# Splitting the attention branch's input pair by pair, sigmoids in pairs, and new memory offsets in a hybrid encoder layer

## The chip, the core and the metric

The kernel runs on one core of a Trainium2 chip. A core has five engines that work at the same time, each with its own queue of instructions: TensorE (PE; its weight loads are shown apart as PEld), VectorE (DVE), ScalarE (ACT), GpSimd (POOL) and SyncE (SP, which here only issues DMAs). They wait for one another on semaphores. Operands of TensorE lie in SBUF, a memory of 128 partitions; its results go to PSUM, of which this kernel uses eight banks of 128 x 512 float32. The metric is the device time of one execution in microseconds; lower is better.

## What is computed

One layer of a bidirectional hybrid encoder on x of 512 tokens by 1024 channels, in float32:

```python
proj = u @ w_in
q, k, v, z, xbc, dt_raw, gate = jnp.split(proj, offs, axis=-1)
ya = neighbourhood_attention(q, k, v, rpb) @ w_attn_br      # 16 heads of 64
...
ys = y.reshape(bsz, s, D_INNER) @ w_ssd_br                  # two directions of Mamba-2
gates = jax.nn.sigmoid(gate + b_gate).reshape(bsz, s, N_BRANCH, D_MODEL)
merged = gates[:, :, 0] * ya + gates[:, :, 1] * ys
mix = merged @ w_o
...
h = layer_norm(DN_ALPHA * h + mix, ln1_g, ln1_b)
h = layer_norm(DN_ALPHA * h + jnp.square(jax.nn.relu(h @ w1)) @ w2, ln2_g, ln2_b)
```

Here u is a first layer norm of x. Attention works on a grid of 8 rows by 64 columns of tokens: each query sees a window of 8 rows by 16 columns, with a bias from rpb.

## The kernel before

**Products in three parts.** TensorE multiplies in a format shorter than float32, so each operand is split into a high part (a copy into that format, on ScalarE) and a low part (the difference, on VectorE or GpSimd), and each product is three matmuls: high by high, high by low, low by high (`mm3`, L352 to L354). `weights` and `split_weights` (L326 to L350) load a slab of weights (tag `ws`) and split it into `wh` and `wl`, in two halves, two buffers of each tag. In names, h and l at the end stand for the two parts: aTh and aTl, hTh and hTl, mgh and mgl.

**Stages.** The first layer norm and the SSD branch run to 498 us; their order is written by a planner (`Plan`, `slab`, `z_project`, `group_slabs`), which sorts operations by costs and due times. What follows is ordered by a tile scheduler from the order of the code and the buffers: the projection of v (498 to 555 us), the 16 attention heads in eight pairs, the projection of the attention branch (`ps_abr`, 718 to 758 us), gates and merge, w_o, the second layer norm, and the feed-forward (from about 854 us), whose second product uses Strassen's scheme and loads the squared activations `sq..h` and `sq..l` as its stationary operand.

**The heads** (loop over `pr`, L1147 to L1265). Each pair projects q and k, copies them into qf, qs, kf, kh and klz, and then does two heads. For a head: scores into two banks (`pss`), maximum with bias on VectorE (L1218, the result's sign turned at L1222), four exps on ScalarE (L1224), sums and normalisation on VectorE (L1226, L1228), transposes on TensorE into `tp_p` (L1239), their split into `pth` (ScalarE, L1243) and `ptl` (VectorE, L1244), ten matmuls with the values into `po` (L1251, L1252), a copy `low` (ScalarE, L1262) and a sum into `aT` (VectorE, L1265). `po` has one bank, so a head's product waits for the sum of the head before it. The split values lie in one tile `vhl`.

**Around the last heads.** TensorE has other matmuls to do beside the heads: the gate projections `ps_g..`. Gates with d2 = 1 (`merge_gates`, L1052 to L1062, called at L1267) have four of them, each with a sigmoid on ScalarE (L1060). Exp and sigmoid need different tables of ScalarE, so a change between them shows as an ACT_TABLE_LOAD. After the last head, with the heads' pools closed, a new pool holds aTh and aTl: eight copies (L1276) and eight differences (L1277), one for each pair of heads. Then come the eight rows of `ps_abr` (L1281 to L1292), each of 8 x 3 matmuls over k, and their copies `ya`. The code that places memory puts small unused tiles (`gc_pad`, `ge_pad`, `rx_pad`) between others, which set the byte offset of what follows.

Of the kernel before, what the change touches and what calls it, by code (L numbers as in the profile page):

```python
# [54 lines left out]
CC_ID = 0  # L55
CC_TF = 128
CC_TB = 256
CC_MI = 384
CC_M0 = 640
CC_N = 896  # L60
# [12 lines left out]
class Plan:  # L73
# [239 lines left out]
def encoder_layer(ctx, tc, x, w_in, w_attn_br, w_ssd_br, w_o, w_ff1, w_ff2, pcols, rows64,  # L313
# [31 lines left out]

    def weights(parts, nk, ncol, name, eng=nc.vector, pool=None, after=None):
        hi = (pool or wp).tile([P, nk, ncol], F32R, tag="wh", name=f"wh_{name}")
        lo = (pool or wp).tile([P, nk, ncol], F32R, tag="wl", name=f"wl_{name}")
        return split_weights(parts, nk, ncol, name, hi, lo, eng, pool, after)

    def mm3(o, lh, ll, rh, rl, start, stop):
        nc.tensor.matmul(o, lh, rh, start=start, stop=False)  # L352
        nc.tensor.matmul(o, ll, rh, start=False, stop=False)  # L353
        nc.tensor.matmul(o, lh, rl, start=False, stop=stop)  # L354

# [240 lines left out]

    load(("cst", 0), 1.1, cst[:, P:CC_N], consts[:, P:CC_N], 5.0)
    r64 = gcp.tile([P, 2, 64], F32, name="r64")
# [452 lines left out]

    def merge_gates(d2, br):  # L1052

        wg = weights([(w_in, 0, OFF_G + br * D + d2 * 256, 256)], KD, 256, f"g{d2}_{br}")
        gt = gep.tile([P, 2, S], F32, tag="gt", bufs=4, name=f"gt{d2}_{br}")
        for j in range(2):
            d = 2 * d2 + j
            ps = psx.tile([P, S], F32, tag="mm", bufs=BANKS["mm"], name=f"ps_g{d}_{br}")
            project(ps, wg, j * P)
            nc.scalar.activation(gt[:, j, :], ps, AF.Sigmoid,  # L1060
                                 bias=pc[:, PC_BG + br * KD + d : PC_BG + br * KD + d + 1])
        return gt  # L1062
# [45 lines left out]

    vhl = vpp.tile([P, 4, NH // 2, 4, HD], F32R, name="vhl")

# [32 lines left out]

    klz = atp.tile([P, 2, S], F32R, name="klz")
    nc.gpsimd.memset(klz.bitcast(F32), 0.0)

    def q_views(src, dst):  # L1147
# [5 lines left out]
                + [(s3[:, :, 56:64][:, :, ::-1], dst[:, 0, :, 8:16]),  # L1153
                   (s3[:, :, 0:8][:, :, ::-1], dst[:, 0, :, 0:8])])

    for pr in range(NH // 2):
# [25 lines left out]
        for hh in range(2):  # L1182
# [65 lines left out]
            def pv(b, w0, nw, m0, start, stop):  # L1248
                th, tl = (t[:, b % 2, w0 : w0 + nw, :] for t in pts[b // 2])
                v = vhl[:, b, pr, 2 * hh : 2 * hh + 2, :]  # L1250
                nc.tensor.matmul(po[:, m0 : m0 + nw, :], v, th, start=start, stop=False)  # L1251
                nc.tensor.matmul(po[:, m0 : m0 + nw, :], v, tl, start=False, stop=stop)  # L1252

# [12 lines left out]

    gates.append([merge_gates(1, 0), merge_gates(1, 1)])  # L1267
    at.__exit__(None, None, None)
    vpool.__exit__(None, None, None)
    dump("aT", aT)  # L1270
    agp = tc.tile_pool(name="ag", bufs=1, reuse_waits="tile")
    ag = agp.__enter__()
    aTh = ag.tile([P, KD, S], F32R, name="aTh")
    aTl = ag.tile([P, KD, S], F32R, name="aTl")
    for k in range(KD):
        ins = nc.scalar.activation(aTh[:, k], aT[:, k], AF.Copy)  # L1276
        nc.vector.tensor_tensor(out=aTl[:, k], in0=aT[:, k], in1=aTh[:, k].bitcast(F32),  # L1277
                                op=ALU.subtract)
# [3 lines left out]
    for d2 in range(4):  # L1282
# [3 lines left out]
        for j in range(2):  # L1286
            d = 2 * d2 + j
            ps = psx.tile([P, S], F32, tag="mm", bufs=BANKS["mm"], name=f"ps_abr{d}")
            for k in range(KD):
                mm3(ps, wa[0][:, k, j * P : (j + 1) * P], wa[1][:, k, j * P : (j + 1) * P],  # L1290
                    aTh[:, k, :], aTl[:, k, :], k == 0, k == KD - 1)
            nc.scalar.activation(ya[:, d, :], ps, AF.Copy)  # L1292
    agp.__exit__(None, None, None)

# [78 lines left out]
    for t2 in range(2):  # L1373
# [41 lines left out]
    def parts(name, shape):  # L1415

        turn["parts"] += 1
        if turn["parts"] % 3 == 0:
            return third(w3p, name, shape)
        return [wp.tile(shape, F32R, tag=n, name=f"{n}_{name}") for n in ("wh", "wl")]  # L1420

# [275 lines left out]
```

## Time and profile before

| what | value |
|---|---|
| median of three runs | 1206.2 us (1204.68 to 1206.78) |
| the profiled execution's own time | 1207.45 us |
| its span in the trace | 1205.7 us |
| mean clock granted to TensorE | 0.995 |
| instructions | 16822 |

The span goes from the first to the last event in the trace; the 1.75 us more in the execution's own time lie around it. The page's slices divide the span into 40 equal parts of 30.1 us, and a digit is the busy share in tenths. In a timeline each row has start, duration, engine, line and operation, output and inputs, and in brackets how long the engine had been idle before it and what released it. Matmuls are pipelined: the duration of one (0.39 us for 512 columns) is longer than the step from one start to the next, and what a stream of them costs is read from the starts.

### The profile page before, as it was taken

How to read it: one execution, taken by the hardware profiler on the slowest of the kernel's cores; microseconds unless marked ns; L12 is line 12 of the kernel's file. 1: busy time of each engine (PE TensorE's matmuls, PEld its weight loads, DVE VectorE, ACT ScalarE, POOL GpSimd, SP SyncE). 2: the span in 40 equal slices, each digit the busy share in tenths (PEclk: the TensorE clock that was granted, in tenths of full speed). 3: DMA queues.
4: the chain of work that ended last, by engine and by line, in shares of the span. 5: the costliest groups of instructions: out<-in, count | busy, mean ns of one | idle time of the engine just before them, and what ended most of it. 6: DMA issues, size and time to landing. Idle time of an engine off the chain costs nothing.

```text
span 1205.7 us, 16822 instructions
## 1 busy us (share of the span) xinstructions
PE 1172.6 (97%) x6306; PEld 1004.4 (83%) x6306; DVE 780.4 (65%) x1427; ACT 608.9 (51%) x1012; POOL 541.9 (45%) x588
## 2 busy tenths in 40 slices
PE   5999999999999999999999989999999999999996
PEld 5988898989888888788888878889988888878885
DVE  7758475666666665434788975356772566398856
ACT  4576573836355563324667882342254454365410
POOL 1158977777788767303666730015153131221000
PEclk9999999999999999999999989999999999999998
DMA  7144243333333341233423323344238886778511
GB/s 231 54 144 140 88 140 105 107 117 128 105 105 112 117 138 70 71 105 89 110 60 81 84 101 109 105 145 134 72 105 207 214 202 180 189 205 216 162 49 52
DMA packets 131169, 149.21 MB, mean 124 GB/s; under 512 B 22928, under 2 KB 105488, under 8 KB 131088
## 3 DMA queue, kind: packets, MB, share of 16 engines
q1 hardware_dynamic: 118032, 113.54, 30.4%
q0 software_dynamic: 13056, 34.61, 11.8%
q8 instruction: 49, 0.80, 0.3%
q14 instruction: 32, 0.26, 0.1%
HBM read 145.90 MB, written 2.23 MB: 123 GB/s over the span
## 4 chain that ended last, share of the span: by engine, by line
PE 85%; DVE 5%; ACT 3%; DMA 3%; issue 3%; POOL 1%; SPq 0%; DVEq 0%; POOLq 0%; ACTq 0%
PE ps_f L354 8%; PE ps_f L353 8%; PE ps_f L352 8%; PE ps_x L354 5%; PE ps_x L352 5%; PE ps_x L353 5%; PE ps_z L352 3%; PE ps_z L353 3%; PE ps_z L354 3%; PE yd L932 2%; DMA w2r<-in_w_ff 2%; PE ps_sbr L352 2%; PE ps_sbr L354 2%; PE ps_sbr L353 2%; PE ps_g L352 2%
## 5 line engine op out<-in xcount | busy, mean ns | idle before, releaser
L741 DVE SCALAR_TENSOR_TENSOR cv<-ps_x,pc,cv 128x511 f32<-128x511 f32 (+1 forms) x128 | 95.8, 748 | 26.9 <-ACT cv L733 23.3
L353 PE MATMUL ps_f<-h1Th,wl_f 128*128 128x512 f32 (+1 forms) x288 | 104.7, 366 | 0.0
L352 PE MATMUL ps_f<-h1Th,wh_f 128*128 128x512 f32 (+1 forms) x288 | 104.3, 366 | 0.0
L354 PE MATMUL ps_f<-h1Tl,wh_f 128*128 128x512 f32 (+1 forms) x288 | 103.3, 367 | 1.1 <-DVE h1Tl L429 1.1
L1468 DVE TENSOR_TENSOR wl_f<-w2r,wh_f 128x1024 fp32r<-128x1024 f32 x42 | 49.8, 1220 | 64.2 <-ACT wh_f L1467 64.2
L352 PE MATMUL ps_z<-wh_z,hTh 128*128 128x256 f32 x256 | 75.9, 296 | 0.0
L354 PE MATMUL ps_z<-wl_z,hTh 128*128 128x256 f32 x256 | 72.4, 283 | 0.0
L353 PE MATMUL ps_z<-wh_z,hTl 128*128 128x256 f32 x256 | 72.3, 283 | 0.0
L1462 POOL DMA_DIRECT2D w2r<-in_w_ff x30 | 36.3, 1416 | 70.2 <-DMA w2r<-in_w_ff 46.2
L352 PE MATMUL ps_f<-wh_f,sqh 128*128 128x512 f32 x168 | 66.0, 396 | 0.7 <-ACT sqh L1467 0.7
L353 PE MATMUL ps_f<-wh_f,sql 128*128 128x512 f32 x168 | 66.2, 395 | 0.2 <-DVE sql L1468 0.2
L354 PE MATMUL ps_f<-wl_f,sqh 128*128 128x512 f32 x168 | 66.1, 395 | 0.0
L1048 DVE TENSOR_TENSOR ysacc<-ps_sbr,ysacc 128x512 f32<-128x512 f32 x56 | 38.5, 689 | 40.5 <-PE ps_sbr L354 40.3
L342 DVE TENSOR_TENSOR wl_f<-ws_f,wh_f 128x1024 fp32r<-128x1024 f32 x36 | 46.7, 1333 | 24.2 <-ACT wh_f L341 24.1
L353 PEld LDWEIGHTS ps_f<-h1Th,wl_f 128*128 128x128 f32 x288 | 54.2, 188 | 8.9
L354 PEld LDWEIGHTS ps_f<-h1Tl,wh_f 128*128 128x128 f32 x288 | 53.3, 188 | 10.0 <-DVE h1Tl L429 1.3
L352 PEld LDWEIGHTS ps_f<-h1Th,wh_f 128*128 128x128 f32 x288 | 54.1, 188 | 8.9
L1321 POOL TENSOR_TENSOR gt<-gt,ysacc 128x512 f32<-128x512 f32 x8 | 12.8, 1601 | 107.2 <-ACT gt L1060 99.1
L1467 ACT ACTIVATE wh_f<-w2r 128x1024 fp32r<-128x1024 f32 x42 | 42.5, 1052 | 34.4 <-DMA w2r<-in_w_ff 22.0
L352 PE MATMUL ps_x<-hTh,wh_bc 128*128 128x512 f32 (+1 forms) x144 | 56.9, 395 | 1.6 <-ACT wh_bc L471 1.6
L1451 POOL DMA_DIRECT2D w2r<-in_w_ff x18 | 16.1, 896 | 92.3 <-DVE wl_f L1468 55.8
L352 PE MATMUL ps_sbr<-yTh,wh_sbr 128*128 128x512 f32 x128 | 55.6, 434 | 1.2 <-DVE ysacc L1048 0.6
(327 smaller groups left out, 3900.2 us busy)
## 6 DMA issues: line engine op xcount, KB each, us to landing
ws_f<-in_w_ff SPq DMA_DIRECT2D x20, 1024.0 KB
w2r<-in_w_ff POOLq DMA_DIRECT2D x18, 1024.0 KB, 7.3
bc<-acs_d SPq DMA_DIRECT2D x32, 512.0 KB
w2r<-in_w_ff POOLq DMA_DIRECT2D x30, 512.0 KB, 8.6
ws_bc<-in_w_in SPq DMA_DIRECT2D x16, 512.0 KB
ws_x<-in_w_in SPq DMA_DIRECT2D x8, 1024.0 KB
ws_z<-in_w_in SPq DMA_DIRECT2D x8, 1024.0 KB
ws_g<-in_w_in SPq DMA_DIRECT2D x8, 1024.0 KB
```

Source lines behind the costliest of these rows:

```text
L342: (eng[i] if isinstance(eng, tuple) else eng).tensor_tensor(out=lo[:, k], in0=st[:, k], in1=hi[:, k].bitcast(F32), op=ALU.subtract)
L352: nc.tensor.matmul(o, lh, rh, start=start, stop=False)
L353: nc.tensor.matmul(o, ll, rh, start=False, stop=False)
L354: nc.tensor.matmul(o, lh, rl, start=False, stop=stop)
L741: op("DVE", 0.75, lambda j=j, o=o, n=n: nc.vector.scalar_tensor_tensor(out=acc()[:, o], in0=ps()[:, n], scalar=tap(j), in1=acc()[:, o], op ...
L932: nc.tensor.matmul(yd()[:, c % 2, h * HD : (h + 1) * HD], bc()[:, 1, h, :], xtok()[:, c, h * HD : (h + 1) * HD], start=True, stop=True)
L1048: op("DVE", 0.69, lambda d=d, ps=ps: nc.vector.tensor_tensor(out=ysacc[:, d, :], in0=ps(), in1=ysacc[:, d, :], op=ALU.add), r=[(ps.name, 0 ...
L1321: nc.gpsimd.tensor_tensor(out=g1, in0=g1, in1=ysacc[:, d, :], op=ALU.mult)
L1451: load = nc.gpsimd.dma_start(t, rows(i, n, c))
L1462: nc.gpsimd.dma_start(t, rows(i, n, c, k), accum_op=ALU.add)
L1467: nc.scalar.activation(hi[:, k], x, AF.Copy)
L1468: nc.vector.tensor_tensor(out=lo[:, k], in0=x, in1=hi[:, k].bitcast(F32), op=ALU.subtract)
```

## The change

It has four parts.

1. **The split of the branch's input.** `vhl` becomes two tiles of four pairs each. After the fourth pair the first one is no longer read, and aTh takes its place. The copies of aTh are issued during the last four pairs, two in each (`high(k)`). The eight parts of aTl take the places of qf, kf, kh, klz and qs as the last pair leaves them. The heads' pools close behind the projection. Two matmuls (row 0 at k = 6, row 1 at k = 0) are tied behind the last head's last matmul. The rows' banks alternate between the tags "so" and "mm".
2. **Sigmoids in pairs.** The two projections of a gate with d2 = 1 go into banks of two tags, and the first sigmoid is tied behind the second projection; for the second gate both are tied behind the last head.
3. **Margins.** The tiles wh and wl become 2112 columns wide, and some slabs start 16 columns (64 bytes) in: the first slabs of B, C and x, all slabs of z, and the first two of the feed-forward. `ge_pad` goes from 24 to 56 columns. By the program's addresses the squared activations go from 128 to 0 bytes past a multiple of 256, mgh and mgl from 96 to 224, the shifted slabs from 0 to 64.
4. **Constants.** The two triangular matrices move from the constants' tile to a pool that is given back, and their load is a DMA of its own.

The core of the diff:

```diff
+    def wide(t, nk, shift=0):
+        return t[:, shift : shift + 2048].rearrange("p (k c) -> p k c", k=nk)
...
-        hi = (pool or wp).tile([P, nk, ncol], F32R, tag="wh", name=f"wh_{name}")
-        lo = (pool or wp).tile([P, nk, ncol], F32R, tag="wl", name=f"wl_{name}")
+            hi, lo = [wide(wp.tile([P, 2112], F32R, tag=n, name=f"{n}_{name}"), nk, shift)
+                      for n in ("wh", "wl")]
...
-        wh, wl = slab(f"z{g}", [(w_in, 0, OFF_Z + g * 256, 256)], KD, 256, (nc.gpsimd, nc.gpsimd))
+        wh, wl = slab(f"z{g}", [(w_in, 0, OFF_Z + g * 256, 256)], KD, 256, (nc.gpsimd, nc.gpsimd), 16)
...
-    def merge_gates(d2, br):
+    def behind(ins, other, why):
+        tc.add_manual_dep(ins.ins, other.ins.name, mybir.DependencyInfo(
+            mybir.DependencyClass.Sync, mybir.DependencyReason.DATA), reason=why)
+
+    def merge_gates(d2, br, tags=None, after=None):
...
+        if tags:
+            for x in sig if after else sig[:1]:
+                behind(x, after or done, "one change of the table")
...
-    vhl = vpp.tile([P, 4, NH // 2, 4, HD], F32R, name="vhl")
+    vhl = [vpp.tile([P, 4, NH // 4, 4, HD], F32R, tag=f"vhl{i}", name=f"vhl{i}") for i in range(2)]
...
+    def high(k):
+        return nc.scalar.activation(aTh[:, k], aT[:, k], AF.Copy)
...
-    gates.append([merge_gates(1, 0), merge_gates(1, 1)])
-    at.__exit__(None, None, None)
-    vpool.__exit__(None, None, None)
-    dump("aT", aT)
-    agp = tc.tile_pool(name="ag", bufs=1, reuse_waits="tile")
-    ag = agp.__enter__()
-    aTh = ag.tile([P, KD, S], F32R, name="aTh")
-    aTl = ag.tile([P, KD, S], F32R, name="aTl")
+        if pr == 3:
+            aTh = vpp.tile([P, KD, S], F32R, tag="vhl0", name="aTh")
+        elif pr > 3:
+            for k in (2 * (pr - 4), 2 * (pr - 4) + 1):
+                ins = high(k)
+
+    gates.append([merge_gates(1, 0, ("cb", "mm")), merge_gates(1, 1, ("mm", "cb"), last)])
+
+    aTl = []
+    for tag, n in (("qf", 1), ("kf", 1), ("kh", 2), ("klz", 2), ("qs", 2)):
+        t = atp.tile([P, n, S], F32R, tag=tag, name=f"aTl_{tag}")
+        aTl.extend(t[:, i] for i in range(n))
     for k in range(KD):
-        ins = nc.scalar.activation(aTh[:, k], aT[:, k], AF.Copy)
-        nc.vector.tensor_tensor(out=aTl[:, k], in0=aT[:, k], in1=aTh[:, k].bitcast(F32),
+        nc.vector.tensor_tensor(out=aTl[k], in0=aT[:, k], in1=aTh[:, k].bitcast(F32),
                                 op=ALU.subtract)
...
+                if (d, k) in ((0, 6), (1, 0)):
+                    behind(first, last, "the last head")
...
-    gep.tile([P, 24], F32, name="ge_pad")
+    gep.tile([P, 56], F32, name="ge_pad")
```

**Where instructions stand now.** Names carry the head's or row's number (tp_p15_0 is the first transposition of head 15). First TensorE, from the second transposition of head 14 to the first of head 15, before:

```order
L1239 MATMUL tp_p14_1_6826<-cst_81,sc14_6790 128x128 x4
L352 MATMUL ps_g3_1_7026<-hTh_69,wh_g1_1_6991 128x512
L353 MATMUL ps_g3_1_7026<-hTh_69,wl_g1_1_6992 128x512
L354 MATMUL ps_g3_1_7026<-hTl_70,wh_g1_1_6991 128x512
...
L1239 MATMUL tp_p15_0_6894<-cst_81,sc15_6867 128x128 x4
```

and now:

```order
L1263 MATMUL tp_p14_1_6836<-cst_81,sc14_6800 128x128 x4
L1319 MATMUL ps_abr0_7086<-aTh_5953,wh_abr0_7078 128x512
L1322 MATMUL ps_abr0_7086<-aTh_5953,wl_abr0_7079 128x512
L1323 MATMUL ps_abr0_7086<-aTl_qf_7064,wh_abr0_7078 128x512
...
L1323 MATMUL ps_abr0_7086<-aTl_klz_7067,wh_abr0_7078 128x512
L1263 MATMUL tp_p15_0_6904<-cst_81,sc15_6877 128x128 x4
```

Twelve matmuls of the last gate projection stood there; now it is 18 of the branch's row 0 (k = 0 to 5), and the gate's 24 are done ahead of the second transposition of head 14.

ScalarE from head 14's exps to the first split of head 15, before:

```order
L1262 ACTIVATE low12_6601<-po12_6590 64x512
L1243 ACTIVATE pth13_1_6663<-tp_p13_1_6658 128x512
L1060 ACT_TABLE_LOAD
L1060 ACTIVATE gt1_1_6999<-ps_g2_1_7000,pc_82 128x512
L1224 ACT_TABLE_LOAD
L1224 ACTIVATE sc15_6867,sums15_6869<-sc15_6867,mx15_6868 128x256 x4
L1243 ACTIVATE pth14_0_6822<-tp_p14_0_6817 128x512
L1262 ACTIVATE low13_6678<-po13_6667 64x512
L1243 ACTIVATE pth14_1_6831<-tp_p14_1_6826 128x512
L1060 ACT_TABLE_LOAD
L1060 ACTIVATE gt1_1_6999<-ps_g3_1_7026,pc_82 128x512
L1243 ACTIVATE pth15_0_6899<-tp_p15_0_6894 128x512
```

and now, from the copy of head 13 on:

```order
L1286 ACTIVATE low13_6686<-po13_6675 64x512
L1267 ACTIVATE pth14_1_6841<-tp_p14_1_6836 128x512
L1178 ACTIVATE aTh_5953<-aT_4692 128x512
L1267 ACTIVATE pth15_0_6909<-tp_p15_0_6904 128x512
L1286 ACTIVATE low14_6856<-po14_6845 64x512
L1267 ACTIVATE pth15_1_6918<-tp_p15_1_6913 128x512
L1286 ACTIVATE low15_6933<-po15_6922 64x512
L1079 ACT_TABLE_LOAD
L1079 ACTIVATE gt1_1_7011<-ps_g2_1_7012,pc_83 128x512
L1079 ACTIVATE gt1_1_7011<-ps_g3_1_7038,pc_83 128x512
L1178 ACTIVATE aTh_5953<-aT_4692 128x512
```

The second gate's two sigmoids, with one table load in place of the two before them and the one back to exp, stand behind the last head, the last aTh behind them; aTh[6] stands ahead of head 15's first split.

VectorE around the normalisation of head 14, before:

```order
L1226 RECIPROCAL sums14_6792<-sums14_6792 128x4
L1228 TENSOR_SCALAR sc14_6790<-sc14_6790,sums14_6792 128x256 x4
L1265 TENSOR_TENSOR aT_4690<-po12_6590,low12_6601 64x8x16 x3
L1265 TENSOR_TENSOR aT_4690<-po12_6590,low12_6601 64x8x8 x2
L1244 TENSOR_TENSOR ptl13_1_6664<-tp_p13_1_6658,pth13_1_6663 128x512
```

and now:

```order
L1250 RECIPROCAL sums14_6802<-sums14_6802 128x4
L1304 TENSOR_TENSOR aTl_kh_7066<-aT_4692,aTh_5953 128x512 x2
L1304 TENSOR_TENSOR aTl_klz_7067<-aT_4692,aTh_5953 128x512
L1252 TENSOR_SCALAR sc14_6800<-sc14_6800,sums14_6802 128x256 x4
L1304 TENSOR_TENSOR aTl_klz_7067<-aT_4692,aTh_5953 128x512
L1289 TENSOR_TENSOR aT_4692<-po12_6598,low12_6609 64x8x16 x3
L1289 TENSOR_TENSOR aT_4692<-po12_6598,low12_6609 64x8x8 x2
L1268 TENSOR_TENSOR ptl13_1_6672<-tp_p13_1_6666,pth13_1_6671 128x512
```

Four parts of aTl stand among head 14's steps; head 15's maxima follow behind these rows in both.

More of the change, by code (lines that the diff above doesn't have):

```diff
@@ L55 @@
 CC_ID = 0
[L56 to L59, printed above, removed]
+CC_MI = 128
+CC_M0 = 384
+CC_TF = 640
+CC_TB = 768
 CC_N = 896
@@ L344, in split_weights, with weights @@
         return hi, lo
-    def weights(parts, nk, ncol, name, eng=nc.vector, pool=None, after=None):
-        hi = (pool or wp).tile([P, nk, ncol], F32R, tag="wh", name=f"wh_{name}")
-        lo = (pool or wp).tile([P, nk, ncol], F32R, tag="wl", name=f"wl_{name}")
+    def wide(t, nk, shift=0):
+        return t[:, shift : shift + 2048].rearrange("p (k c) -> p k c", k=nk)
+    def weights(parts, nk, ncol, name, eng=nc.vector, pool=None, after=None, shift=0):
+        if pool:
+            hi, lo = [pool.tile([P, nk, ncol], F32R, tag=n, name=f"{n}_{name}") for n in ("wh", "wl")]
+        else:
+            hi, lo = [wide(wp.tile([P, 2112], F32R, tag=n, name=f"{n}_{name}"), nk, shift)
+                      for n in ("wh", "wl")]
         return split_weights(parts, nk, ncol, name, hi, lo, eng, pool, after)
@@ L353, in mm3 @@
         nc.tensor.matmul(o, ll, rh, start=False, stop=False)
-        nc.tensor.matmul(o, lh, rl, start=False, stop=stop)
+        return nc.tensor.matmul(o, lh, rl, start=False, stop=stop)
     def rsqrt(pool, v, n, name, keep=None, eng=nc.vector):
@@ L594, in encoder_layer, with load_cst @@
                w=[(dtps.name, half)])
-    load(("cst", 0), 1.1, cst[:, P:CC_N], consts[:, P:CC_N], 5.0)
+    def load_cst():
+        nc.sync.dma_start(tris, consts[:, CC_TF:CC_N])
+        nc.sync.dma_start(cst[:, P:CC_TF], consts[:, P:CC_TF])
+    op("SP", 1.1, load_cst, r=[("behind", 0)], w=[("cst", 0)], at=5.0)
     r64 = gcp.tile([P, 2, 64], F32, name="r64")
@@ L1130, in encoder_layer @@
         for b in range(4):
-            prs = slice(4 * s, 4 * s + 4)
             pv4 = pss[b].rearrange("p (r h q) -> p r h q", r=4, h=2)
-            hi = vhl[:, b, prs, 0:4:3, :]
+            hi = vhl[s][:, b, :, 0:4:3, :]
             nc.scalar.activation(hi, pv4, AF.Copy)
-            nc.vector.tensor_tensor(out=vhl[:, b, prs, 1:3, :], in0=pv4, in1=hi.bitcast(F32),
+            nc.vector.tensor_tensor(out=vhl[s][:, b, :, 1:3, :], in0=pv4, in1=hi.bitcast(F32),
                                     op=ALU.subtract)
@@ L1249, in pv @@
                 th, tl = (t[:, b % 2, w0 : w0 + nw, :] for t in pts[b // 2])
-                v = vhl[:, b, pr, 2 * hh : 2 * hh + 2, :]
+                v = vhl[pr // 4][:, b, pr % 4, 2 * hh : 2 * hh + 2, :]
                 nc.tensor.matmul(po[:, m0 : m0 + nw, :], v, th, start=start, stop=False)
-                nc.tensor.matmul(po[:, m0 : m0 + nw, :], v, tl, start=False, stop=stop)
+                return nc.tensor.matmul(po[:, m0 : m0 + nw, :], v, tl, start=False, stop=stop)
             pv(0, 0, 2, 0, True, False)
@@ L1258, in encoder_layer @@
             pv(3, 0, 1, 3, False, False)
-            pv(3, 1, 1, 0, False, True)
+            last = pv(3, 1, 1, 0, False, True)
             low = atp.tile([P, 4, P], F32, tag="low", name=f"low{h}")
@@ L1287, in encoder_layer @@
             d = 2 * d2 + j
-            ps = psx.tile([P, S], F32, tag="mm", bufs=BANKS["mm"], name=f"ps_abr{d}")
+            tag = ("so", "mm")[d2 % 2]
+            ps = psx.tile([P, S], F32, tag=tag, bufs=BANKS[tag], name=f"ps_abr{d}")
             for k in range(KD):
-                mm3(ps, wa[0][:, k, j * P : (j + 1) * P], wa[1][:, k, j * P : (j + 1) * P],
-                    aTh[:, k, :], aTl[:, k, :], k == 0, k == KD - 1)
+                w = [t[:, k, j * P : (j + 1) * P] for t in wa]
+                first = nc.tensor.matmul(ps, w[0], aTh[:, k, :], start=k == 0, stop=False)
+                if (d, k) in ((0, 6), (1, 0)):
+                    behind(first, last, "the last head")
+                nc.tensor.matmul(ps, w[1], aTh[:, k, :], start=False, stop=False)
+                nc.tensor.matmul(ps, w[0], aTl[k], start=False, stop=k == KD - 1)
             nc.scalar.activation(ya[:, d, :], ps, AF.Copy)
-    agp.__exit__(None, None, None)
+    at.__exit__(None, None, None)
+    vpool.__exit__(None, None, None)
     rx0 = tc.tile_pool(name="rx0", bufs=1, side="right", reuse_waits="tile")
@@ L1419, in parts @@
             return third(w3p, name, shape)
[L1420 removed]
+        return [wide(wp.tile([P, 2112], F32R, tag=n, name=f"{n}_{name}"), shape[1])
+                for n in ("wh", "wl")]
     def raw(name):
```

43 lines of the change are left out of this document (24 added, 19 removed).

## The prediction, made before the changed kernel was run

> **What bounds the kernel now.** I read the page first: which engine is full, and which engine the chain of waits runs on.
>
> ```profile
> PE 1172.6 (97%) x6306; PEld 1004.4 (83%) x6306; DVE 780.4 (65%) x1427; ACT 608.9 (51%) x1012; POOL 541.9 (45%) x588
> PEclk9999999999999999999999989999999999999998
> PE 85%; DVE 5%; ACT 3%; DMA 3%; issue 3%; POOL 1%; SPq 0%; DVEq 0%; POOLq 0%; ACTq 0%
> ```
>
> TensorE is busy for 1172.6 us of the 1205.7 us span and carries 85% of the chain. So only three things can shorten the kernel: fewer of its 33 us of idle time, less time at a reduced clock, or a shorter step from one matmul to the next. The clock row has a dip in slice 24, which is 693 to 723 us, the end of the attention heads. Next come the windows of that place, and of one other place with a long wait (stretch, length, then the busy us of TensorE, its weight loads, VectorE, ScalarE and GpSimd with their instructions, TensorE's clock, DMA share, GB/s):
>
> ```profile
> 500.00:510.00 10.00, 8.21 (x35) 6.15 (x35) 6.84 (x12) 2.01 (x2) 2.51 (x2) 1.00 0.32 105
> ...
> 700.00:710.00 10.00, 9.94 (x54) 8.11 (x53) 7.03 (x27) 9.27 (x21) 3.85 (x6) 1.00 0.32 107
> 710.00:720.00 10.00, 6.79 (x33) 5.47 (x34) 6.32 (x21) 6.41 (x11) 1.29 (x1) 0.74 0.15 54
> ```
>
> Between 710 and 720 us TensorE is busy for 6.79 of 10 us, and the clock is 0.74. Just before, ScalarE is nearly full (9.27 of 10). TensorE's timeline shows where the time is lost (start, duration, what; in brackets the idle time and its releaser):
>
> ```profile
> 711.01 0.36 PE L1251 MATMUL po<-pth,vhl 128*128 128x256 f32 x1 [0.46 <-DVE aT L1265]
> ...
> 712.50 0.62 PE L1239 MATMUL tp_p<-cst,sc 128*128 128x128 f32 x4
> 714.46 0.36 PE L1251 MATMUL po<-pth,vhl 128*128 128x256 f32 x1 [1.33 <-DVE aT L1265]
> ...
> 718.10 0.79 PE L352 MATMUL ps_abr<-aTh,wh_abr 128*128 128x512 f32 x1 [1.38 <-ACT aTh L1276]
> 718.69 0.63 PE L353 MATMUL ps_abr<-aTh,wl_abr 128*128 128x512 f32 x1
> ...
> 721.68 0.40 PE L352 MATMUL ps_abr<-aTh,wh_abr 128*128 128x512 f32 x1
> 721.92 0.40 PE L353 MATMUL ps_abr<-aTh,wl_abr 128*128 128x512 f32 x1
> ```
>
> Three waits, 0.46 + 1.33 + 1.38 = 3.17 us: for two heads' softmax, then for the split of the branch's input. From 718.69 to 721.68 seven steps take 0.427 us each, from there on 0.24 and less. These are half-clock steps. The eight from 718.10 on take 3.58 where eight at 0.228 (the step of the full clock) take 1.82: about 1.8 us lost. The head's own ten matmuls lose some 0.7 more.
>
> **The tail, part by part.** ScalarE and VectorE feed these waits. ScalarE's groups from 685 to 717 us (operation, count, busy us and mean ns, idle time before):
>
> ```profile
> L1224 ACT ACTIVATE sc<-sc,mx 128x256 f32<-128x256 f32 x12 | 6.0, 499 | 0.7 <-DVE mx L1222 0.6
> L1060 ACT ACT_TABLE_LOAD x4 | 5.1, 1283 | 0.1
> L1243 ACT ACTIVATE pth<-tp_p 128x512 fp32r<-128x512 f32 x8 | 4.7, 590 | 0.1
> L1224 ACT ACT_TABLE_LOAD x3 | 3.8, 1283 | 0.1
> L1262 ACT ACTIVATE low<-po 64x512 f32<-64x512 f32 x5 | 3.0, 591 | 3.6 <-PE po L1252 2.8 <-ACT pth L1243 0.7
> L1060 ACT ACTIVATE gt<-ps_g,pc 128x512 f32<-128x512 f32 x4 | 2.8, 688 | 0.0
> ```
>
> and places of the two timelines:
>
> ```profile
> 717.42 4.27 ACT L1276 ACTIVATE aTh<-aT 128x512 fp32r<-128x512 f32 x8
> ...
> 731.01 0.60 ACT L1292 ACTIVATE ya<-ps_abr 128x512 f32<-128x512 f32 x1 [2.12 <-PE ps_abr L354]
> ```
> ```profile
> 705.57 0.17 DVE L1222 TENSOR_SCALAR mx<-mx 128x4 f32<-128x4 f32 x1
> ...
> 708.10 1.15 DVE L1228 TENSOR_SCALAR sc<-sc,sums 128x256 f32<-128x256 f32 x4
> ...
> 713.37 0.94 DVE L1265 TENSOR_TENSOR aT<-po,low 64x128 f32<-64x128 f32 x5 [0.59 <-ACT low L1262]
> ...
> 718.45 4.91 DVE L1277 TENSOR_TENSOR aTl<-aT,aTh 128x512 fp32r<-128x512 f32 x8
> ```
>
> Removed: four of ScalarE's seven table loads (4 x 1.28 = 5.1 us of ScalarE), and from the path behind the last head seven of the eight aTh (4.27/8 = 0.53 us each) and seven aTl (4.91/8 = 0.61 each). None of that is TensorE's time in itself; it counts only as far as the three waits shrink.
>
> Added to ScalarE's and VectorE's queues ahead of head 15: aTh[5], and aTl[2] to [5] between head 14's sums and head 15's maxima, 4 x 0.61 = 2.4 us. I walked the new order with these durations. Head 15's maximum, ready at 705.74 before, comes at 708.8: VectorE's aTl and a sum that waits for a later exp cost 3 us. The four exps end at 711.4 (4 x 0.5 us, and a pth between them), the normalised scores at 712.8 (before 708.10 + 1.15 = 709.25). So the last head starts its transposes some 3.2 us later. What TensorE does meanwhile is the point: 18 matmuls of the projection's first row (k = 0 to 5) stand there now, 18 x 0.228 = 4.1 us, from 708.9 to 713.0, with all of their inputs split by then. No wait is left ahead of the transposes.
>
> Then: transposes to 713.5, head 14's value product (711.01 to 712.50 before) to 715.4, the last transposes, and on ScalarE and VectorE pth, low, aT (0.6, 0.6, 0.9 us by the rows) and ptl, with aTh[6] and aTl[6] among them until head 15's product can start, at 717.15 (before 714.46). In the walk that is the one wait left, about 1.7 us in place of 3.17. The product ends at 718.8. Of the 48 matmuls of the first two rows 30 are left: 30 x 0.228 = 6.8, end 725.6. Their last inputs, aTh[7] and aTl[7], come behind one table load and two sigmoids (1.28 + 1.4 + 0.53 + 0.61 after low15), at about 723.2, and the seven groups placed ahead (24 x 0.228 = 5.5 us from 718.8) cover that with 1.1 us to spare.
>
> Against 731.0 before that is -5.4 us at the full clock. If the clock halves again for as many steps (+1.8), it is -3.5. I take **-3.5**, since 1.7 us of wait stand among transposes and short matmuls, as the 1.33 us wait did, right behind which the 0.2 us steps of half clock begin. Against it: the window 500:510 has 1.79 us of idle time at clock 1.00,
>
> ```profile
> 508.99 1.16 PE L352 MATMUL ps_v<-wh_v,hBh 128*128 128x512 f32 x4 [1.21 <-ACT wh_v L341]
> ```
>
> with a wait of 1.21 us in it, among full matmuls. So the bound lies between, and both ends stay in the range: -5.5 to -0.5, the last if the chain of the last head is 3 us longer than walked.
>
> The Trainium skill, page "TensorE: Matmul & The Clock Gate", section "HAM oscillation — how this bites in real kernels", puts the rule as no idle gap of TensorE over about 3.4 us. By it no wait here would cost clock, and the tail would give the full-clock sum. The rows above do not agree: no gap is over 1.38 us, and the steps were halved.
>
> **Squares (ge_pad 24 to 56 columns).** The squared activations, which the second feed-forward product loads as its stationary operand, move in memory from the middle of a 256-byte block to a block's start, where the first product's operands stand. One timeline has both, 14 steps of the first product and 12 of the second:
>
> ```profile
> 1053.75 0.39 PE L352 MATMUL ps_f<-h1Th,wh_f 128*128 128x512 f32 x1
> ...
> 1056.92 0.39 PE L354 MATMUL ps_f<-h1Tl,wh_f 128*128 128x512 f32 x1
> 1058.03 0.50 PE L352 MATMUL ps_f<-wh_f,sqh 128*128 128x512 f32 x1 [0.72 <-ACT sqh L1467]
> ...
> 1059.09 0.39 PE L354 MATMUL ps_f<-wl_f,sqh 128*128 128x512 f32 x1
> ...
> 1061.88 0.40 PE L354 MATMUL ps_f<-wl_f,sqh 128*128 128x512 f32 x1
> ```
>
> 3.17/14 = 0.2264 against 2.79/12 = 0.2325 us: 6 ns a step. The count comes from the windows of the high half alone (two of three matmuls read it):
>
> ```profile
> 940.00:1018.40 78.40, 45.38 (x144) 27.13 (x144) 11.23 (x17) 10.37 (x17) 1.00 0.73 200
> 1018.40:1058.00 39.60, 15.48 (x49) 9.04 (x48) 2.14 (x4) 2.48 (x4) 1.00 0.85 185
> 1058.00:1156.00 98.00, 46.20 (x144) 27.04 (x144) 12.03 (x18) 10.48 (x17) 1.00 0.66 183
> ```
>
> 216 matmuls before 1018.4 and 216 after 1058 run at TensorE's pace. Between them the chain of waits goes through the weights' DMA (the 0.72 us wait at 1058.03 is its end), so the 74 there gain nothing. 432 x 6.1 ns = 2.6 us. The shapes' median durations (below, 389 and 393 ns) give 4 ns, so 1.7. I take **-2.2**, ends 0 and -2.6.
>
> **Margins of the weights and of mgh.** The weights of z (there the moving operand), of the first slabs of B, C and x and of the first two slabs of the feed-forward (there the stationary one) go from a block's start to 64 bytes past it; mgh and mgl, w_o's stationary operand, from 96 to 224.
>
> ```profile
> L352 PE MATMUL ps_f<-h1Th,wh_f x288: 277/389/398, 854.1 to 1146.5; 128*128 128x512 f32 x112, 128*128 128x256 f32 x32
> L352 PE MATMUL ps_z<-wh_z,hTh x256: 277/283/681, 51.4 to 470.4; 128*128 128x256 f32 x128
> L352 PE MATMUL ps_f<-wh_f,sqh x168: 390/393/501, 946.4 to 1152.0; 128*128 128x512 f32 x168
> L352 PE MATMUL ps_o<-wh_o,mgh x128: 277/280/368, 807.0 to 853.7; 128*128 128x256 f32 x128
> ```
>
> None of these rows has an operand at 64 or 224 bytes. The nearest: z now, 283 ns, all at a block's start, and w_o, 280, whose stationary operand is 96 off. If z takes on the 3 ns, 3 x 256 x 3 ns = -2.3 us, and with the first slabs -2.7. If an offset costs as it does the squares, 6 ns on all 1,536 matmuls concerned (768 of z, 384 of w_o, 192 of the first x slabs, 192 of the first feed-forward slabs), it is +9.4. I take a third of the gain, **-0.8**, being nearest to the rows of the same 256 columns.
>
> **The rest, +0.3** (0 to +0.5): aTh[0] to [4], 0.53 us each, go into ScalarE's queue while TensorE still has its other matmuls to do (9.94 of 10 us in 700:710); the constants come in two DMAs; the residual rows' loads wait behind four weight loads, and VectorE's normalisation of them moves behind the weights of the third pair of gates, where the walk still has those of the next before their use.
>
> Sum: -3.5 - 2.2 - 0.8 + 0.3 = **-6.2** against the profiled run's 1207.45 us, which is 1.25 above the median of 1206.2. On the median: **1200.0 us**.
>
> **Rivals.**
> - The clock stays full in the tail: -5.4 in place of -3.5, -8.1, 1198.1. For it the 1.21 us wait at clock 1.00 and a single wait in place of three; against it the 1.33 us one.
> - Addresses do not matter: the squares' 6 ns come from something else that they have (other weights for each step, the DMA traffic of that stage, 0.73 busy), and so do z's 3 ns. Then -3.2, 1203.0. Against it: the first product's steps, 2 us earlier under the same traffic, are at 0.2264. The Trainium skill, the same page, section "Step-by-step: what each phase is for", has a read port of its own for loading the stationary operand, so that loading the next one takes nothing from the running matmul; by that rule squares and margins give nothing, and the trace's two step lengths, 0.2264 and 0.2325, do not bear it out.
> - The last head's chain takes the fill back: VectorE's four aTl delay head 15 by 3.5 us more than walked (a normalisation under a GpSimd operation can cost more than the 1.15 us of 708.10), so the wait ahead of the transposes returns and the tail gives 0: -2.7, 1203.5.
> - The weights' stream sets the end of the feed-forward: what is won before 1058 is given back in a longer wait there, and only the second half of the squares is left, 216 x 5.5 ns: -1.2, 1205.0. Against it, the chain of waits enters that DMA from a split on ScalarE, one that TensorE's release of a buffer starts:
>
> ```profile
> 1018.46 1.07 ACT wh_f L1467
> ...
> 1042.03 12.34 DMA w2r<-in_w_ff
> ```
> - Slower: the offsets of 64 and 224 bytes cost 6 ns on each of the 1,536 matmuls, +9.4 in place of -0.8. Sum +4.0, 1210.2. It decides from (3.5 + 2.2 - 0.3)/1,536 = 3.5 ns on. Against it: w_o at 96 is no slower than z at 0.
> - Nothing of it acts: the places are taken later than planned and the waits come back, within 1 us of before.
>
> **How the numbers follow.** Chances: forecast 0.36 (its own range 1198.5 to 1202), full clock 0.18, addresses 0.13, last head 0.13, stream 0.07, nothing 0.06, slower 0.07. 0.2%, about what a measurement of this kernel can tell from no change, is 2.4 us, so faster means below 1203.8: forecast, full clock, addresses and half of the last head's case, 0.73. Slower is 0.07, the rest 0.20. The range goes from the full clock with z's 2.7 us (1198.1 - 1.9), 0.4 for the squares' far end and 0.3 for a rest that costs nothing: 1195.5, to 1205.0, the stream's case.
>
> **What would show it.** Right: matmuls of ps_abr ahead of the last head's transposes, three table loads from 685 us to the end of the heads, one wait of 1 to 2 us before the last product, the second ya some 3.5 us earlier, squares at 227 ns a step, z at 280. Wrong: a wait ahead of the last transposes, half-clock steps beyond eight, squares still at 232, z or w_o above 283, or a longer wait at the squares' first step near 1058.

## The result, and the profile after

| kernel | median, us | range | runs |
|---|---|---|---|
| before | 1207.37 | 1204.68 to 1212.77 | 6 |
| changed | 1198.03 | 1197.46 to 1201.02 | 6 |

The ratio is 0.9926, with a 95% interval of 0.9907 to 0.9945: 8.9 us faster (6.6 to 11.2). The forecast was 6.2, with 1195.5 to 1205.0 as its range. The profiled execution took 1199.65 us, 7.8 less than that of before. One of the twelve executions of squares_only below took 1678.16 us at a mean granted clock of 0.657, and its ratio leaves that one out. First the changed kernel's page, with the engines and the granted clock:

```profile
PE 1163.5 (97%) x6306; PEld 997.6 (83%) x6306; DVE 779.5 (65%) x1427; ACT 602.4 (50%) x1008; POOL 543.5 (45%) x588
PEclk9999999999999999999999999999999999999999
PE 85%; DVE 6%; DMA 3%; ACT 3%; issue 2%; POOL 0%; DVEq 0%; POOLq 0%; ACTq 0%
```

TensorE's busy time fell by 9.1 us (1172.6 to 1163.5) with the same 6306 instructions: its idle time rose a little (33.1 to 34.4), so the gain lies in shorter steps, those of the half clock among them. The clock's dip in slice 24 is gone. The windows of the end of the heads:

```profile
700.00:710.00 10.00, 10.00 (x54) 8.29 (x53) 7.74 (x25) 3.90 (x11) 4.85 (x5) 1.00 0.33 107
710.00:720.00 10.00, 7.97 (x47) 6.46 (x46) 6.59 (x21) 6.05 (x15) 0.00 (x0) 1.00 0.00 0
720.00:730.00 10.00, 10.00 (x46) 8.30 (x46) 6.80 (x12) 8.54 (x11) 3.00 (x2) 1.00 0.06 15
```

TensorE is busy 7.97 us instead of 6.79 between 710 and 720 us, at full clock. Its timeline there:

```profile
709.42 0.62 PE L1263 MATMUL tp_p<-cst,sc 128*128 128x128 f32 x4
709.80 0.48 PE L1319 MATMUL ps_abr<-aTh,wh_abr 128*128 128x512 f32 x1
...
713.74 0.39 PE L1323 MATMUL ps_abr<-aTl_klz,wh_abr 128*128 128x512 f32 x1
713.98 0.60 PE L1263 MATMUL tp_p<-cst,sc 128*128 128x128 f32 x4
715.22 0.36 PE L1275 MATMUL po<-pth,vhl 128*128 128x256 f32 x1 [0.65 <-DVE aT L1289]
...
718.69 0.35 PE L1275 MATMUL po<-pth,vhl 128*128 128x256 f32 x1 [1.35 <-DVE aT L1289]
...
720.05 0.44 PE L1319 MATMUL ps_abr<-aTh,wh_abr 128*128 128x512 f32 x1
```

Eighteen matmuls of the projection fill 709.80 to 713.98 us, and no wait stands ahead of head 15's transposes. Two waits are left, 0.65 + 1.35 = 2.0 us, where there were three of 3.17; the projection goes on right behind the last head. VectorE, which releases both, shows why the first is there:

```profile
702.85 1.68 DVE L1304 TENSOR_TENSOR aTl_kh<-aT,aTh 128x512 fp32r<-128x512 f32 x2
704.45 0.95 DVE L1304 TENSOR_TENSOR aTl_klz<-aT,aTh 128x512 fp32r<-128x512 f32 x1
...
706.38 0.68 DVE L1304 TENSOR_TENSOR aTl_klz<-aT,aTh 128x512 fp32r<-128x512 f32 x1
...
709.92 0.17 DVE L1246 TENSOR_SCALAR mx<-mx 128x4 f32<-128x4 f32 x1
...
712.93 1.14 DVE L1252 TENSOR_SCALAR sc<-sc,sums 128x256 f32<-128x256 f32 x4
714.08 0.99 DVE L1289 TENSOR_TENSOR aT<-po,low 64x128 f32<-64x128 f32 x5
```

The four aTl took 1.68 + 0.95 + 0.68 = 3.3 us, not 2.4, and head 15's maximum is ready at 710.09, not 708.8. Head 13's sum `aT` (714.08) stands behind it, and frees the one bank of `po` late.

The shapes' durations (min, median, max in ns) on line 359, which was line 352 before:

```profile
L359 PE MATMUL ps_f<-h1Th,wh_f x288: 276/389/396, 849.9 to 1138.9; 128*128 128x512 f32 x112, 128*128 128x256 f32 x32
L359 PE MATMUL ps_z<-wh_z,hTh x256: 276/279/680, 50.8 to 470.9; 128*128 128x256 f32 x128
L359 PE MATMUL ps_f<-wh_f,sqh x168: 389/389/502, 941.4 to 1144.3; 128*128 128x512 f32 x168
L359 PE MATMUL ps_o<-wh_o,mgh x128: 277/280/364, 803.1 to 849.5; 128*128 128x256 f32 x128
```

Squares went from 393 to 389, z from 283 to 279, w_o stayed at 280.

### The profile page after: what moved, and what is told of

The parts are those of the page before. It is cut to its first block, busy times and chain, and to the rows that moved or that the text cites. A ratio compares the mean times of both kernels' runs of the same rounds, so it can differ in the third digit from the quotient of the medians.

```text
span 1197.9 us, 16822 instructions
## 1 busy us (share of the span) xinstructions
PE 1163.5 (97%) x6306; PEld 997.6 (83%) x6306; DVE 779.5 (65%) x1427; ACT 602.4 (50%) x1008; POOL 543.5 (45%) x588
## 4 chain that ended last, share of the span: by engine, by line
PE 85%; DVE 6%; DMA 3%; ACT 3%; issue 2%; POOL 0%; DVEq 0%; POOLq 0%; ACTq 0%
PE ps_f L361 8%; PE ps_f L359 8%; PE ps_f L360 8%; PE ps_x L359 5%; PE ps_x L361 5%; PE ps_x L360 5%; PE ps_z L359 3%; PE ps_z L360 2%; PE ps_z L361 2%; PE yd L945 2%; DMA w2r<-in_w_ff 2%; PE ps_sbr L359 2%; PE ps_sbr L361 2%; PE ps_sbr L360 2%; PE ps_g L359 2%
```

## The experiments

Steps below are means of the time from one matmul's start to the next of the same output, over all of a trace, with waits left out. Times are compared by the ratio to the kernel before that ran beside them (0.001 is 1.2 us).

| run | median, us | before beside it | ratio, 95% interval |
|---|---|---|---|
| squares_only | 1204.96 | 1207.9 | 0.9983 [0.9971, 0.9996] |
| tail_only | 1205.05 | 1207.9 | 0.9981 [0.9972, 0.9989] |
| no_margins | 1202.02 | 1207.9 | 0.9960 [0.9946, 0.9974] |
| margins_everywhere | 1211.33 | 1207.9 | 1.0030 [1.0016, 1.0044] |
| z_plain | 1200.01 | 1207.12 | 0.9940 [0.9928, 0.9953] |
| pairs_only | 1205.59 | 1207.12 | 0.9988 [0.9978, 0.9997] |
| split_only | 1203.15 | 1207.12 | 0.9964 [0.9952, 0.9977] |
| offset_sweep | 1200.48 | 1207.12 | one run |
| changed_again | 1197.96 | 1206.61 | 0.9926 [0.9912, 0.9941] |
| z_at_192 | 1198.7 | 1206.61 | 0.9930 [0.9917, 0.9943] |
| z_at_192_mgh_at_64 | 1198.15 | 1206.61 | 0.9926 [0.9913, 0.9939] |

**squares_only**: the kernel before, with one number changed.

```diff
-    gep.tile([P, 24], F32, name="ge_pad")
+    gep.tile([P, 56], F32, name="ge_pad")
```

> The kernel before with ge_pad at 56 columns, nothing else; the order of instructions on every engine is that of before. Squares start at 0 mod 256, mgh at 224. Theory (address): 504 steps of the second feed-forward product go from 232.5 to 227 ns, 432 of them at TensorE's pace, so -2.4 us against before (-1.7 to -2.6). Rival (the step length belongs to that stage's DMA traffic or its changing weights): the steps stay at 232 to 233 ns and the time within 0.5 us of before.

2.1 us faster (0.5 to 3.5). The squares' step went from 232.7 to 226.8 ns. A pad of 32 columns does it under the same traffic, so the address is the cause; the rival falls. The pad also takes mgh and mgl from 96 to 224, and w_o's step went from 117.5 to 116.6 ns; some 0.4 us of the gain are w_o's by its steps. This trace shows a second thing. It has the order of before and the same waits at the end of the heads, yet another clock:

```profile
714.97 0.36 PE L1251 MATMUL po<-pth,vhl 128*128 128x256 f32 x1 [1.34 <-DVE aT L1265]
...
717.88 0.50 PE L352 MATMUL ps_abr<-aTh,wh_abr 128*128 128x512 f32 x1 [1.38 <-ACT aTh L1276]
718.21 0.39 PE L353 MATMUL ps_abr<-aTh,wl_abr 128*128 128x512 f32 x1
718.44 0.40 PE L352 MATMUL ps_abr<-aTh,wh_abr 128*128 128x512 f32 x1
```

The steps are at 0.23 us, where the profile of before had 0.427. So the half clock does not come in every execution. But it is not rare in the kernel before. The traces tell how to count it: each has some 6 to 9 us of half clock at its end; those with no more have a mean granted clock of 0.997 or 0.998, those with one more stretch of 6.8 us 0.995, those with two more 0.992 or 0.993. Of the 55 executions of the kernel before that ran beside these experiments, 32 are at 0.995 or less (mean 0.9951); of twelve of the changed kernel, four (mean 0.9964). Where in an execution it came, the mean does not tell: four of the thirteen traces have such a stretch near 16 us.

**tail_only**: the changed kernel, with the addresses of before.

```diff
     def wide(t, nk, shift=0):
+        shift = 0
...
-    gep.tile([P, 56], F32, name="ge_pad")
+    gep.tile([P, 24], F32, name="ge_pad")
```

> The changed kernel with the addresses of before (ge_pad 24, no 64-byte margins); the order of instructions is that of the changed kernel. Theory: only the last heads' region gains. The matmuls of row 0 fill the time ahead of head 15, waits of about 2 us in place of 3.2 us, no half-clock steps: -4 us against before (-3.4 to -5.5), and no waits in group 5 of the SSD branch around 327 and 350 us, if those come from TensorE running ahead with shorter z steps. Rival (the tail gives nothing and the addresses carry the whole gain): within 1 us of before.

2.3 us faster than before (1.3 to 3.4): less than the 3.4 to 5.5 that were expected. The waits are the changed kernel's, and none stands near 327 or 350 us.

**no_margins**: `shift = 0` alone.

> The changed kernel without the 64-byte margins (ge_pad stays 56); order as in the changed kernel. Theory: tail and squares without the margins, -6.3 us against before, that is 2 to 4 us slower than the changed kernel (768 steps of z x 2.5 ns and 384 of the first slabs x 5.5 ns = 4.0 us, less what waits behind them give back). Rival (the margins are given back wholly in the waits of group 5 of the SSD branch): as fast as the changed kernel, within 1 us.

4.8 us faster than before, 4.1 behind the changed kernel: the margins' steps in full (768 x 2.5 and 384 x 5.6 ns = 4.1 us). The rival falls. Its trace has the half clock, with the changed kernel's order, from the second wait on, in windows of 5 us:

```profile
715.00:720.00 5.00, 2.97 (x21) 2.28 (x19) 4.41 (x14) 2.31 (x4) 0.00 (x0) 0.98 0.00 0
720.00:725.00 5.00, 5.00 (x21) 4.33 (x20) 0.99 (x5) 3.10 (x5) 0.46 (x1) 0.68 0.00 0
```

Of the nine traces with the changed kernel's order, this is the one with it.

**margins_everywhere**: `shift = 16` for every slab.

> The changed kernel with the 64-byte margin on every slab that has one to give, order as in the changed kernel. 2112 matmuls of 512 columns get their stationary operand at 64 mod 256, 648 their moving one. Theory A (a stationary operand at 64 saves 5 ns a step, as the 256-column steps went from 119.7 to 114): up to 2112 x 5 = 10 us faster than the changed kernel, steps at 222 ns. Theory B (512-column steps lose from any offset of the stationary operand, as at 128): steps at 232 ns, 12 us slower than the changed kernel. Theory C (512 columns hide it): steps at 227 ns, same time.

Slower than before, and 12.6 us behind the changed kernel: theory B. The same 64 bytes that shorten most steps of 256 columns lengthen those of 512:

```profile
L360 PE MATMUL ps_x<-hTh,wh_bc x144: 276/394/796, 15.0 to 442.7; 128*128 128x512 f32 x112, 128*128 128x256 f32 x32
L360 PE MATMUL ps_g<-hTh,wh_g x128: 392/394/504, 65.5 to 811.4; 128*128 128x512 f32 x128
```

394 instead of 389 ns; by the starts 233.3 instead of 227.3 for the gates. By the program's addresses it is 2304 matmuls, not the 2112 expected, that have their stationary operand at 64: at 4 to 6.7 ns each by output. A moving operand at 64 costs too: v's steps of 512 columns went from 226.7 to 228.7 ns, the squares' from 226.8 to 229.6, and half of w_o's of 256 columns, with mgh at 224, from 116.6 to 119.9. All of it sums to some 15 us, above the 12.6 measured but inside its interval of some 3 us. The slower rival of the prediction has a real mechanism, mostly on the other shape than the one it named.

**z_plain**: z alone without its margin (the last argument of its slab).

```diff
-        wh, wl = slab(f"z{g}", [(w_in, 0, OFF_Z + g * 256, 256)], KD, 256, (nc.gpsimd, nc.gpsimd), 16)
+        wh, wl = slab(f"z{g}", [(w_in, 0, OFF_Z + g * 256, 256)], KD, 256, (nc.gpsimd, nc.gpsimd))
```

> The changed kernel with z's weights back at 0 mod 256, the first slabs' margins kept; order as in the changed kernel. Theory (the two waits of group 5, 0.6 and 1.3 us near 327 and 350 us, come from z's shorter steps): z's 768 steps go back to 119.7 ns, the waits are gone, the time is within 1 us of the changed kernel. Rival (the waits are chance, or come from the first slabs): waits stay in some traces and the time is 1.9 us longer.

1.7 us behind the changed kernel, 2.4 ahead of no_margins. The waits of group 5 are gone, as the theory had it, and the time is nearer to the rival. But 1.7 us is within the noise here (both ratios' intervals overlap by far); z's steps, 119.7 against 117.2 ns, are 768 x 2.5 = 1.9 us, and how much of that reaches the time these runs do not settle.

**pairs_only**: all copies of aTh tied behind the last head, so that nothing can fill.

```diff
-            for k in (2 * (pr - 4), 2 * (pr - 4) + 1):
-                ins = high(k)
+            pass
...
+    for k in range(KD):
+        ins = high(k)
+        behind(ins, last, "all behind the last head")
```

> The changed kernel with all eight copies of aTh tied behind the last head, so that none of the projection can fill the time ahead of head 15; sigmoids in pairs and addresses as in the changed kernel. Theory (the fill carries the tail's gain): the projection starts after the split as before, the wait of about 1.4 us in front of it is back, 2 to 3.5 us slower than the changed kernel. Rival (the table loads carry it): within 1 us of the changed kernel.

7.5 us behind the changed kernel, twice what the theory had. TensorE's waits:

```profile
711.90 0.66 PE L1263 MATMUL tp_p<-cst,sc 128*128 128x128 f32 x4 [1.44 <-DVE ptl L1268]
713.02 0.36 PE L1275 MATMUL po<-pth,vhl 128*128 128x256 f32 x1 [0.46 <-DVE aT L1289]
716.47 0.36 PE L1275 MATMUL po<-pth,vhl 128*128 128x256 f32 x1 [1.34 <-DVE aT L1289]
721.82 0.79 PE L1321 MATMUL ps_abr<-aTh,wh_abr 128*128 128x512 f32 x1 [3.83 <-ACT aTh L1178]
```

The second gate's sigmoids and their table load, which the change puts behind the last head, now stand ahead of the split: 3.83 us of wait where before had 1.38, and with it the half clock (0.50 in the window of 5 us):

```profile
720.00:725.00 5.00, 3.18 (x8) 2.50 (x9) 3.20 (x4) 5.00 (x10) 2.96 (x2) 0.50 0.00 0
```

Pairing alone would cost time at that place; it is the split that gives TensorE something to do there.

**split_only**: the gates of d2 = 1 as before.

```diff
-    gates.append([merge_gates(1, 0, ("cb", "mm")), merge_gates(1, 1, ("mm", "cb"), last)])
+    gates.append([merge_gates(1, 0), merge_gates(1, 1)])
```

> The changed kernel with the gates of d2 = 1 as before (no pairs, no ties of the sigmoids); split and addresses as in the changed kernel. The scheduler then orders the gates' matmuls a little differently, row 0 of the projection still fills the time ahead of head 15. Theory: the four table loads come back into ScalarE's queue ahead of the last head, its product waits 1 to 2 us longer, 1 to 2 us slower than the changed kernel. Rival (ScalarE hides them): within 0.5 us.

4.6 us behind the changed kernel (2.6 in the profiled executions), where 1 to 2 were expected. ScalarE has seven table loads again, and TensorE waits at a place of its own:

```profile
700.73 1.28 ACT L1248 ACT_TABLE_LOAD   x1
...
705.36 1.28 ACT L1079 ACT_TABLE_LOAD   x1
706.66 0.69 ACT L1079 ACTIVATE gt<-ps_g,pc 128x512 f32<-128x512 f32 x1
707.37 1.28 ACT L1248 ACT_TABLE_LOAD   x1
```
```profile
702.56 0.39 PE L1276 MATMUL po<-ptl,vhl 128*128 128x256 f32 x1 [2.27 <-DVE ptl L1268]
...
720.44 0.36 PE L1275 MATMUL po<-pth,vhl 128*128 128x256 f32 x1 [1.35 <-DVE aT L1289]
```

Since the scheduler orders the heads' work anew here, the 4.6 us are those of the whole arrangement, not of the table loads alone. Taken from tail_only, both parts together are worth 2.3 us; so by the ratios either of them alone, arranged like this, is slower than neither (the split alone by 2.3 us, no more than its interval).

**offset_sweep**: `8 * g` columns for z and for the slabs of groups 1 to 7; 8, 24, 32 and 48 for the four slabs of 256 columns.

> The changed kernel with another margin for each slab, order as in the changed kernel: z of group g has its moving operand (256 columns) at 32 g bytes past a block of 256, the slabs of B, C and x of groups 1 to 7 their stationary operand (512 columns) at 32 g, those of group 0 (256 columns) at 32 and 96, the first two of the feed-forward at 128 and 192. It measures the steps by offset: theory, with 512 columns every stationary offset but 0 costs 5 to 6 ns, with 256 columns every one but 0 saves 2 to 6 ns. Rival: the cost goes with the distance to the block's start, so 32 and 224 are nearly free. The time itself is expected 2 to 5 us above the changed kernel (576 steps of 512 columns x 6 ns = 3.5 us).

| offset, bytes | 0 | 32 | 64 | 96 | 128 | 160 | 192 | 224 |
|---|---|---|---|---|---|---|---|---|
| 512 columns, stationary | 227.3 | 233.1 | 233.3 | 233.9 | 232.8 | 233.5 | 228.9 | 233.3 |
| 256 columns, moving (z) | 119.9 | 116.8 | 117.8 | 119.9 | 118.7 | 117.5 | 114.5 | 118.4 |
| 256 columns, stationary | 119.8 | 118.2 | 113.7 | 118.5 | 118.1 | | 117.8 | |

(ns a step; the two stationary figures at 0 are the gates here and x in no_margins, that at 64 is x in the changed kernel.) For 512 columns every offset but 0 and 192 costs 6 ns; the rival of a growing distance falls. For 256 columns every stationary offset tried saves something, 64 the most. The time was 2.3 us above the changed kernel's by the ratio, in one run.

The figures for 256 columns, one group or slab each, are not the offset's alone. With z at 64 throughout, group 0 steps at 113.4 ns and groups 1 to 7 at 117.4 to 117.8, in both traces of the changed kernel, in margins_everywhere and in split_only; in pairs_only, with the same addresses, group 0 too is at 117.8. A stream keeps one of these two steps and may leave it behind an interruption. With z's weights and activations all at 0 neither was seen: 119.2 to 120.0 in every group of five traces.

**changed_again, z_at_192, z_at_192_mgh_at_64.** The last two try the sweep's best places.

```diff
-        wh, wl = slab(f"z{g}", [(w_in, 0, OFF_Z + g * 256, 256)], KD, 256, (nc.gpsimd, nc.gpsimd), 16)
+        wh, wl = slab(f"z{g}", [(w_in, 0, OFF_Z + g * 256, 256)], KD, 256, (nc.gpsimd, nc.gpsimd), 48)
...
-    rx0p.tile([P, 8], F32, name="rx_pad")
+    rx0p.tile([P, 48], F32, name="rx_pad")
```

> The changed kernel itself, beside the next two on the same chip. Theory: 9 us (8 to 10) under the kernel before; the wait of 1.3 us near 350 us is in its trace again, since it came in all four traces that had z at 64 in every group, and in none of five with z at 0.

> The changed kernel with z's moving operand at 192 in place of 64 mod 256; order as in the changed kernel. The sweep had 114.5 ns a step at 192 (one group) and 117 to 118 at 64. Theory: 768 x 2.9 ns = 2.2 us fewer in z's own steps, and up to 2.2 us faster than the changed kernel. Rival (TensorE ahead of the SSD branch's other engines gains nothing): the waits of groups 5 and after grow by as much, same time within 0.5 us.

> As the one before, and rx_pad at 48 columns, which puts mgh and mgl (the stationary operand of w_o) from 224 to 64 mod 256; order as in the changed kernel. Theory: 384 steps of 256 columns go from 117 to 114 ns, as the first slabs did at 64: 1.0 us faster than z_at_192. Rival: w_o stays at 117, same time.

The changed kernel gave 0.9926 again, but its trace has no wait near 350 us this time, against what was expected. z at 192 runs at 116.5 ns over all groups (113.5 in group 0, 117.8 in 2 to 4), not at the sweep's 114.5 for group 6, which is here at 117.0: 0.7 x 768 = 0.5 us, and no gain in time. mgh at 64 gives 115.9 instead of 116.6, and the first feed-forward slabs, untouched at 64, went from 114.2 to 117.1 in that kernel, with unchanged addresses: they too mostly ran at the longer of the two steps. No version beats the changed one.

## Why the prediction was right, and where it was off

The sum was 6.2 us and is 8.9. By the ratios, part upon part: tail 2.3 (tail_only), squares 2.5 (no_margins on top of it), first slabs 2.4 (z_plain on top), z 1.7 (changed). That they make 8.9 together is no check, since each is the difference to the one before. The tail's interval is about 1 us to either side, those of squares and first slabs about 2, so that both are barely clear of zero, and z's is over 2, so that z is not. What the steps measured (2.5, 2.1 and 1.9 us, and 0.4 of w_o) bears the sizes out.

- **Tail: forecast 3.5, measured 2.3 (1.3 to 3.4).** The mechanism was right: the matmuls of row 0 fill the time ahead of head 15, and the projection starts without a wait of its own. Its size was not. The walk took 0.61 us for each aTl and had head 15's product start at 717.15; it started at 718.69 (718.61 in tail_only, with the addresses of before), with a second wait of 0.65 that the walk did not have. Two traces without half clock at that place show the size: the projection's second copy `ya` starts at 729.32 us in squares_only, with the order of before, and at 727.32 in tail_only, with the sum `aT` of an earlier head at 676.01 and 675.95. That is 2 us, where the forecast, which kept the half clock on both sides, had 3.5; the late product is most of the difference. Nor did the half clock stay on both sides: of nine traces with the changed order only no_margins has it there. What a rarer half clock adds is at most 0.0011 x 1206 = 1.3 us, an estimate from the mean granted clocks, 0.9961 in tail_only and 0.9950 in the kernel before beside it. The rival "the clock stays full" describes the changed kernel's profile; its 5.4 us was counted against a row with half clock in it (731.01), which not every execution of before has. One reading of the rows was off too: the first two waits of before are for the sum `aT` of the head ahead, by the one bank of `po`, not for a softmax. The wait of the last head's product is 1.33 to 1.35 us in all thirteen traces, whatever was changed around it.
- **Squares: forecast 2.2, measured 2.5 and 2.1.** Right in cause, and in size as far as the intervals tell; both figures hold w_o's 0.4 us, which the prediction had under the margins. The wait at the first squares near 1058 us was longer in this execution (in changed_again it was 0.18). Its end in the changed kernel, where 0.72 and 0.23 stood:

```profile
1051.44 0.50 PE L359 MATMUL ps_f<-wh_f,sqh 128*128 128x512 f32 x1 [1.10 <-ACT sqh L1501]
1052.17 0.50 PE L360 MATMUL ps_f<-wh_f,sql 128*128 128x512 f32 x1 [0.23 <-DVE sql L1502]
```

- **Margins: forecast 0.8, measured 4.1. This is the term that was mis-sized.** It took a third of 2.7, from the 3 ns between the rows of z and w_o, and gave all shapes of 256 columns one figure. Its own 3 ns on the 768 and 384 matmuls would be 3.5 us, not 2.7, and no row supports taking a third. z did what those rows say (119.7 to 117.2, 1.9 us). But the 384 matmuls of the first slabs, whose stationary operand moved, saved 5.6 ns each (119.8 to 114.1), twice the bound. No row of before had a stationary operand at 64 bytes, so the bound from the nearest row was too narrow on that side.
- **The rest: forecast +0.3.** Not tried by itself. tail_only holds it, so the tail's 2.3 us stand against 3.5 - 0.3 = 3.2 of the forecast.
- **Rivals.** That addresses do not matter is refuted by squares_only; that the last head's chain takes all back, by tail_only. The weights' stream took back some 0.4 us at 1051 us in the first profile and nothing in changed_again. The slower one did not come, since w_o's step at 224 was 116.6 ns (117.5 at 96) and the 64 bytes went only to shapes of 256 columns.
- **A wait that nobody forecast.** In the first profile of the changed kernel the SSD branch gives back 1.9 us:

```profile
PE yo L959 <- DVE t L971: 1.3, 1, 1.3
...
PE ps_z L359 <- DVE cv L752: 0.6, 1, 0.6
```

One of these rows or both (who waits, for whom, us in all) come in six of the seven traces with z at 64 or 192 throughout, not in changed_again, and in none of the five with z at 0. So with z shorter TensorE sometimes waits for VectorE in that branch. Which input is late there was not tried and stays open. In the medians little of it is seen.

## What to carry to other kernels

Where TensorE is full, the step from start to start, by shape and by the operands' byte offset within 256, is worth a table: here 2.5 to 6 ns a step were 6.6 of 8.9 us. Try the offset for each shape by itself, and over all groups; the same 64 bytes gained 2.4 us on 384 matmuls, and put on every slab cost 12.6, mostly on 2304 others. And a stall at the end of a stage is filled only if the next stage's input is split early enough and what was put behind it (here the paired sigmoids) has cover: the split without the pairs was 4.6 us worse than both, the pairs without the split 7.5.

## What the runs showed of the hardware

- A stationary operand that starts off a multiple of 256 bytes lengthens the step of 512 columns from 227 to 233 ns (64 and 128 bytes in all traces, six of seven offsets in the sweep) and shortens that of 256 columns from 120 to 114 (at 64) or about 118. At 192 the step of 512 is 228.9. The offset within 256 is not all: with a stationary or a moving operand at 64, a stream of 256 columns runs at 113.4 or at 117.8 ns at the very same addresses (the first slabs of the feed-forward 114.2 and, in the last kernel, 117.1 on the mean). What decides between the two is open. The Trainium skill, page "TensorE: Matmul & The Clock Gate", section "Step-by-step: what each phase is for", gives the gap between matmuls by their columns alone and has the next weights' loading take nothing from the running matmul; these steps do not agree with it.
- TensorE's half clock behind short waits is not a fixed cost of these waits. With the same 1.3 us waits it came in the profile of before and not in that of squares_only. It lasted 6.8 us in the former and about 3.4 us in no_margins. The same page, section "HAM oscillation — how this bites in real kernels", puts the rule as no idle gap of over about 3.4 us; none of these gaps was over 1.38.
